# A decoder trunk on one core: forming p's operands in the values' buffers, and multiplying attention's output matrix in two passes

## The chip, the cores and the metric

The kernel runs on one core of one Trainium2 chip. The metric is the device time of one execution in microseconds (us). Three runs of the kernel before took 1282.44, 1286.07 and 1287.14 us; the median is 1286.07 us. The engines are named as the profile names them: PE (TensorE, matmuls) with PEld (its weight loads), DVE (VectorE), ACT (ScalarE), POOL (GpSimd) and SP (SyncE, which here only issues transfers).

## The reference, cut to what matters

Two layers over 512 tokens of width 1024. Layer 0 is a convolution module, layer 1 differential attention; each is followed by a SwiGLU block and by a gated input p of width 256:

```python
for i in range(DEPTH):                                  # 2 layers
    if i % N_MIXERS == 0:
        h = h + conformer_conv(rms_norm(h, conv_norm_g[j]), ...)
    else:
        h = h + diff_attention(rms_norm(h, attn_norm_g[j]), w_qkv, ..., w_o, ...)
    h = h + swiglu(rms_norm(h, ffn_norm_g[i]), w_gate, w_up, w_down)
    gate = sigmoid(rms_norm(h, ple_norm_g[i]) @ ple_w_gate[i])
    h = h + gate * (p[i] @ ple_w_proj[i])
```

The change lies between the two middle lines of layer 1: the end of `diff_attention`, whose last step is `o.reshape(B, S, N_HEADS * V_DIM) @ w_o` over eight heads of 128 values, and the product `p[1] @ ple_w_proj[1]`, which depends on nothing else and is kept until the last line.

## The kernel before, in words

Activations lie transposed: `h[c]` is a tile of 128 features by 512 tokens, c = 0 to 7. Each product of fp32 numbers is made of three matmuls (`mm3`, L161 to L165): both operands are split into a rounded part `hi` and a rest `lo`, and lo*hi, hi*lo and hi*hi are summed in PSUM. A weight tile goes through `weight()` (L144): SP loads 128 x 1024 numbers (512 KB) into one of two raw buffers (`wraw`), ACT rounds them into `whi` (L156), DVE subtracts to get `wlo` (L158); `whi` and `wlo` have four buffers each.

Layer 1's attention is laid out as six slabs of 512 weight columns (`QKV`: q and k of a pair of heads together, or the values of four heads), each multiplied with four blocks of 128 tokens. Between these matmuls stand the pieces of the attention itself. A block (head, qb) has three of them: `stage_s` (scores into `sc`, L944 and L945, then minimum and bias on DVE, L947, and exp on ACT, L951), `stage_t` (transposes, L964, split on ACT and DVE, L966 and L967) and `stage_a` (times the values, L980 and L981). After a head's fourth block its output is normalised in a tile `D`, and `stage_o` transposes it (L1009) and splits it into the tiles `A` (L177, L178) as operand `ot[head]`. After each token block of a q slab, `unit_end` transposes q and k (L899) and splits them (L907 to L917). The values' splits lie in `B0` to `B7`: `B0` to `B3` hold heads 0 to 3, one tile for each token block, `B4` to `B7` heads 4 to 7. q and k of a pair of heads lie in `C0` to `C5`, two buffers each.

33 of the 96 pieces are left when the last slab ends. They are taken one by one by `step()`. First, p is loaded into the two raw buffers and split into `C0` and `C1` (`pfeatures`, L261 and L262; these buffers become free with the scores of heads 4 and 5); two weight tiles and 48 matmuls give the eight products `pp[m]`, evicted by L275 into `D2`, `D3`, `C2`, `C3` and `C4`, with a `step()` at 24 places. Then `linear` multiplies the output matrix: output tiles m = 0 and 1 together, the others one by one, each over all eight heads; `heads_until(k)` first finishes head k, and `add_attn` (L1077) adds to `h[m]` and prepares the next norm. After it comes the SwiGLU of layer 1.

The source sets only what depends on what. The order on each engine is made by a list scheduler with its own estimate of durations (`schedule_with_timeline_sim=True`), and each engine then runs its instructions in that order. DMA issues stand in SP's queue in such an order too, and one that waits for a buffer holds up those behind it.

Of the kernel before, what the change touches and what calls it, by code (L numbers as in the profile page):

```python
# [13 lines left out]
F32R = mybir.dt.float32r  # L14
AF = mybir.ActivationFunctionType
ALU = mybir.AluOpType
# [4 lines left out]
P = 128  # L21
S = 512
D = 1024
NC = D // P
# [67 lines left out]
def trunk(ctx, tc, xT, pT, wts, diag, dww, vec, rel, onehot, lamv, out):  # L92
    nc = tc.nc
    V, A, G, T = nc.vector, nc.scalar, nc.gpsimd, nc.tensor
# [7 lines left out]
    def sb(shape, tag, bufs, dt=F32):  # L102
        uid[0] += 1
        return pool.tile(shape, dt, tag=tag, name=f"{tag}_{uid[0]}", bufs=bufs)

    def ps(tag, bufs, shape=(P, S)):
        uid[0] += 1
        return psum.tile(list(shape), F32, tag=tag, name=f"{tag}_{uid[0]}", bufs=bufs)

    mm = lambda: ps("mm", 4)  # L110
# [4 lines left out]
    f = lambda ap: ap.bitcast(F32)  # L115
# [16 lines left out]
    t = wk()[:, 0:P]  # L132
# [4 lines left out]
    t = tp()  # L137
# [4 lines left out]
    wnext = [0]  # L142
# [18 lines left out]
    def mm3(acc, a, b, first, last):  # L161
        (ah, al), (bh, bl) = a, b
        T.matmul(acc, al, bh, start=first, stop=False)  # L163
        T.matmul(acc, ah, bl, start=False, stop=False)  # L164
        return T.matmul(acc, ah, bh, start=False, stop=last)  # L165

    def wpart(w, k):
        return tuple(t[:, k * P : (k + 1) * P] for t in w)

    def both(t):  # L170
        return t[:, 0], t[:, 1]


    h = [sb([P, S], f"h{c}", 1) for c in range(NC)]
# [82 lines left out]
    def pfeatures(layer, parts):  # L257
        for k, (hi, lo) in enumerate(parts):
            raw = sb([P, 1024], "wraw", 2)[:, :S]
            nc.sync.dma_start(raw, pT[layer, :, k * S : (k + 1) * S])  # L260
            A.copy(hi, raw)  # L261
            (G if layer == 0 else V).tensor_tensor(lo, raw, f(hi), ALU.subtract)  # L262
        return parts

    ph = pfeatures(0, [(sb([P, S], t, 2, F32R), sb([P, S], t, 2, F32R)) for t in ("wth", "wtl")])
# [3 lines left out]
    def project(ph, m, w, o, step=lambda: None):  # L269

        acc = mm()
        for k in range(2):
            last_product[0] = mm3(acc, wpart(w, 2 * (m % 4) + k), ph[k], k == 0, k == 1)
            step()
        A.copy(o, acc)  # L275
        return o
# [4 lines left out]
    accs = {}  # L281
# [206 lines left out]
    pp = []  # L488
# [57 lines left out]
    def linear(n_in, src, consume, group0=1, before=None, after=None, first=(None,) * 3):  # L546


        m = 0
        while m < NC:  # L550
            g = group0 if m == 0 else 1
            ws = [weight(n_in * P, after=first[i] if m == 0 else None) for i in range(g)]
            accs = [mm() for _ in range(g)]
            for k in range(n_in):
                if before:
                    before(k)
                for w_, a_ in zip(ws, accs):
                    mm3(a_, wpart(w_, k), src[k], k == 0, k == n_in - 1)
                    if after:
                        after()  # L560
            for i in range(g):
                consume(m + i, accs[i])
            m += g
# [245 lines left out]
    for k in range(2):  # L809
        t = tp()  # L810
# [193 lines left out]
    ot = {}  # L1004
# [18 lines left out]
    def take(n):  # L1023
        got, stages[:n] = [s for _, s in stages[:n]], []
        return got

    waiting = None
    for what, at, pace in QKV:
        ws = slab(GLO if at > 0 else 0)
        for tb in range(4):  # L1030
            between = take(3 * pace[tb])
            between += [None] * (6 - len(between))
            if waiting:
                between.append(partial(unit_end, *waiting))
                waiting = None
            if what == "v":
                values(at, ws, tb, between)
            else:
                waiting = unit(at, ws, tb, between)
# [5 lines left out]
    def step():  # L1045
        if stages:
            n, s = stages.pop(0)
            s()
        else:
            n = 99  # L1050
        while done[0] < NH and (n - LA - 3) // 4 > done[0]:
            stage_o(done[0])
            done[0] += 1

    ph = pfeatures(1, [both(sb([P, 2, S], t, 2, F32R)) for t in ("C0", "C1")])
    pp = []
    for m in range(NC):
        if m % 4 == 0:
            w = weight()
        step()  # L1060
        if m < 2:
            o = sb([P, S], f"D{m + 2}", 1)
        elif m % 2 == 0:
            o2 = sb([P, 2, S], f"C{m // 2 + 1}", 2)
            o = o2[:, 0]
        else:
            o = o2[:, 1]
        pp.append(project(ph, m, w, o, step))

    def heads_until(k):  # L1070
        while done[0] <= k:
            step()
# [3 lines left out]
    def add_attn(m, acc):  # L1076
        V.tensor_tensor(h[m], acc, h[m], ALU.add)  # L1077
        norm.chunk(m)

    linear(NC, ot, add_attn, 2, heads_until, step)  # L1080
    n2 = Norm("ple_g1")
    ffn(norm, n2, SPACE[1])

# [131 lines left out]
```

## Time and profile before

| | |
|---|---|
| median of three runs | 1286.07 us |
| the profiled execution | 1285.64 us |
| its span, first to last instruction | 1283.8 us |
| PE / DVE / ACT / POOL busy | 98% / 71% / 48% / 21% of the span |
| mean granted PE clock | 0.986 |
| last slab's tokens end, on PE | 790.6 us from the span's start |
| first matmul of the output matrix | 829.99 us |
| first matmul of the SwiGLU behind it | about 884 us |

Times inside the execution are us from the start of the span. A row of a timeline gives start, duration, engine, line, operation and tiles, and at its end in brackets how long the engine sat idle before and what ended that. A matmul's duration covers its way through the array, so matmuls that follow each other start closer together than they last. A row of the table by stretches gives, for each engine, the busy time in that stretch, then the PE clock that was granted (1.00 is full speed), the share of the DMA engines' time and GB/s.

### The profile page before, as it was taken

How to read it: one execution, taken by the hardware profiler on the slowest of the kernel's cores; microseconds unless marked ns; L12 is line 12 of the kernel's file. 1: busy time of each engine (PE TensorE's matmuls, PEld its weight loads, DVE VectorE, ACT ScalarE, POOL GpSimd, SP SyncE). 2: the span in 40 equal slices, each digit the busy share in tenths (PEclk: the TensorE clock that was granted, in tenths of full speed). 3: DMA queues.
4: the chain of work that ended last, by engine and by line, in shares of the span. 5: the costliest groups of instructions: out<-in, count | busy, mean ns of one | idle time of the engine just before them, and what ended most of it. 6: DMA issues, size and time to landing. Idle time of an engine off the chain costs nothing. (4 is left out here: it accounts for less than half of the span.)

```text
span 1283.8 us, 18407 instructions
## 1 busy us (share of the span) xinstructions
PE 1253.2 (98%) x7056; PEld 1089.0 (85%) x7056; DVE 910.9 (71%) x1470; ACT 614.0 (48%) x1019; POOL 273.5 (21%) x239
## 2 busy tenths in 40 slices
PE   8999899999999999999999998999999999999998
PEld 5888678889899989988788886778888899899887
DVE  6888646785578557776678897946974588558665
ACT  5542445443255325454566766834542355235442
POOL 4645323000000000033335544122000001000030
PEclk8999989999999999999999999999999999999999
DMA  6654313275457545233222221313364466444241
GB/s 236 223 163 158 114 48 115 70 209 142 117 143 187 151 119 137 70 121 101 77 92 87 85 76 51 94 49 120 118 169 139 122 176 173 138 110 118 79 140 66
DMA packets 60164, 157.32 MB, mean 123 GB/s; under 512 B 6403, under 2 KB 11011, under 8 KB 60076
## 3 DMA queue, kind: packets, MB, share of 16 engines
q1 hardware_dynamic: 53344, 135.94, 33.2%
q0 software_dynamic: 4608, 16.78, 8.0%
q10 hardware_dynamic: 2124, 3.43, 0.9%
q8 instruction: 55, 0.90, 0.3%
q14 instruction: 33, 0.27, 0.1%
HBM read 151.91 MB, written 4.21 MB: 122 GB/s over the span
## 5 line engine op out<-in xcount | busy, mean ns | idle before, releaser
L164 PE MATMUL mm<-A,whi 128*128 128x512 f32 (+1 forms) x904 | 312.7, 347 | 0.6 <-DVE A L178 0.3
L163 PE MATMUL mm<-A,wlo 128*128 128x512 f32 (+1 forms) x904 | 308.3, 346 | 4.5 <-DVE wlo L158 2.5
L165 PE MATMUL mm<-A,whi 128*128 128x512 f32 (+1 forms) x904 | 310.0, 344 | 0.0
L156 ACT CAST whi<-wraw 128x1024 fp32r<-128x1024 f32 (+2 forms) x150 | 151.2, 1014 | 233.0 <-PE mm L165 93.4
L158 DVE TENSOR_TENSOR wlo<-wraw,whi 128x1024 fp32r<-128x1024 f32 (+2 forms) x146 | 186.6, 1280 | 65.8 <-ACT whi L156 65.0
L163 PEld LDWEIGHTS mm<-A,wlo 128*128 128x128 f32 x904 | 171.8, 190 | 27.5 <-DVE wlo L158 4.2
L164 PEld LDWEIGHTS mm<-A,whi 128*128 128x128 f32 x904 | 172.1, 190 | 24.5 <-DVE A L178 3.8
L165 PEld LDWEIGHTS mm<-A,whi 128*128 128x128 f32 x904 | 172.1, 190 | 20.4 <-issue 1.0
L164 PE MATMUL mm<-B,whi 128*128 128x512 f32 x352 | 137.3, 391 | 0.0
L650 POOL DMA_DIRECT2D C<-in_wts x32 | 28.1, 880 | 511.4 <-DVE h L761 179.4
L165 PE MATMUL mm<-B,whi 128*128 128x512 f32 x352 | 137.1, 390 | 0.0
L163 PE MATMUL mm<-B,wlo 128*128 128x512 f32 x352 | 134.9, 392 | 0.0
L197 POOL TENSOR_TENSOR acc<-acc,wk 128x512 f32<-128x512 f32 x42 | 65.7, 1564 | 229.6 <-ACT wk L196 122.1
L761 DVE TENSOR_TENSOR h<-mm,h 128x512 f32<-128x512 f32 x48 | 33.0, 687 | 64.8 <-PE mm L165 64.8
L165 PEld LDWEIGHTS mm<-B,whi 128*128 128x128 f32 x352 | 66.1, 188 | 14.4
L163 PEld LDWEIGHTS mm<-B,wlo 128*128 128x128 f32 x352 | 66.1, 188 | 14.0
L164 PEld LDWEIGHTS mm<-B,whi 128*128 128x128 f32 x352 | 66.1, 188 | 13.9
L165 PE MATMUL mm<-whi,A 128*128 128x512 f32 x192 | 75.7, 395 | 0.0
L164 PE MATMUL mm<-wlo,A 128*128 128x512 f32 x192 | 74.9, 395 | 0.0
L163 PE MATMUL mm<-whi,A 128*128 128x512 f32 x192 | 74.8, 396 | 0.0
L222 POOL TENSOR_TENSOR r<-v,mhalf 128x8 f32<-128x8 f32 (+1 forms) x31 | 46.2, 1490 | 117.1 <-DVE v L220 94.6
L643 DVE TENSOR_TENSOR wlo<-wraw,whi 128x1024 fp32r<-128x1024 f32 x32 | 39.2, 1225 | 32.8 <-ACT whi L642 32.8
(269 smaller groups left out, 2700.7 us busy)
## 6 DMA issues: line engine op xcount, KB each, us to landing
wraw<-in_wts SPq DMA_DIRECT2D x162, 512.0 KB, 3.7
C<-in_wts SPq DMA_DIRECT2D x32, 512.0 KB, 4.7
C<-in_wts POOLq DMA_DIRECT2D x32, 512.0 KB, 6.2
bias<-in_wts SPq DMA_DIRECT2D x32, 256.0 KB, 3.8
wraw<-in_wts SPq DMA_DIRECT2D x16, 384.0 KB, 3.1
D<-in_diag SPq DMA_DIRECT2D x22, 256.0 KB, 4.2
C<-in_diag SPq DMA_DIRECT2D x16, 256.0 KB, 4.4
h<-in_xT SPq DMA_DIRECT2D x8, 256.0 KB, 5.2
```

The costliest lines, as they stand in the source:

```text
L156: A.copy(hi[:, cut], raw[:, cut])
L158: eng.tensor_tensor(lo[:, cut], raw[:, cut], f(hi[:, cut]), ALU.subtract)
L163: T.matmul(acc, al, bh, start=first, stop=False)
L164: T.matmul(acc, ah, bl, start=False, stop=False)
L165: return T.matmul(acc, ah, bh, start=False, stop=last)
L197: self.last = self.eng.tensor_tensor(self.acc, self.acc, sq, ALU.add)
L222: last_pow[0] = G.tensor_tensor(r[:, :n], v[:, :n], mhalf[:, :n], ALU.pow)
L643: V.tensor_tensor(lo, raw, f(hi), ALU.subtract)
L650: nc.gpsimd.dma_start(q, wts[i + 2].rearrange("p (a s) -> p a s", a=2), accum_op=ALU.add)
L761: V.tensor_tensor(h[m], acc, h[m], ALU.add)
```

## The change

Three things are done.

1. `pfeatures(1, ...)` is called in the last slab, before its third token block, with `B0` and `B1` as the tiles; the values of heads 0 to 3 there are no longer read then.
2. The first four products `pp[0]` to `pp[3]` are evicted into `B2` and `B3`. After attention, DMAs copy them to `D2`, `D3` and `C2`, where the other products of the old kernel lay.
3. The output matrix is multiplied in two passes of half weight tiles (128 x 512 numbers, 256 KB, `half_weight`): first all eight m over heads 0 to 3, with `step()` after each of the 32 products, each m ending in an addition to `h[m]`; then pairs of m over heads 4 to 7, with the old `add_attn`. The numbers of matmuls are the same; weight loads, casts and splits are 16 halves rather than eight whole tiles, and there are eight additions to `h[m]` more.

```diff
@@ -1028,6 +1028,8 @@
     for what, at, pace in QKV:
         ws = slab(GLO if at > 0 else 0)
         for tb in range(4):
+            if (what, at, tb) == ("q", 3, 2):
+                ph = pfeatures(1, [both(sb([P, 2, S], t, 1, F32R)) for t in ("B0", "B1")])
             between = take(3 * pace[tb])
@@ -1052,20 +1054,14 @@
-    ph = pfeatures(1, [both(sb([P, 2, S], t, 2, F32R)) for t in ("C0", "C1")])
     pp = []
     for m in range(NC):
         if m % 4 == 0:
             w = weight()
         step()
-        if m < 2:
-            o = sb([P, S], f"D{m + 2}", 1)
-        elif m % 2 == 0:
-            o2 = sb([P, 2, S], f"C{m // 2 + 1}", 2)
-            o = o2[:, 0]
-        else:
-            o = o2[:, 1]
-        pp.append(project(ph, m, w, o, step))
+        if m % 2 == 0:
+            o2 = sb([P, 2, S], f"B{m // 2 + 2}", 1) if m < 4 else sb([P, 2, S], f"C{m // 2 + 1}", 2)
+        pp.append(project(ph, m, w, o2[:, m % 2], step))
@@ -1077,7 +1073,43 @@
-    linear(NC, ot, add_attn, 2, heads_until, step)
+    base = wnext[0]
+    wnext[0] += NC
+
+    def half_weight(m, first):
+        raw = sb([P, 1024], "wraw", 2)[:, :S]
+        nc.sync.dma_start(raw, wts[base + m, :, first : first + S])
+        hi = sb([P, 1024], "whi", 4, F32R)[:, :S]
+        lo = sb([P, 1024], "wlo", 4, F32R)[:, :S]
+        A.copy(hi, raw)
+        V.tensor_tensor(lo, raw, f(hi), ALU.subtract)
+        return hi, lo
+
+    for m in range(NC):
+        w = half_weight(m, 0)
+        acc = mm()
+        for k in range(4):
+            heads_until(k)
+            mm3(acc, wpart(w, k), ot[k], k == 0, k == 3)
+            step()
+        V.tensor_tensor(h[m], acc, h[m], ALU.add)
+    for m in range(0, NC, 2):
+        ws = [half_weight(m + i, S) for i in range(2)]
+        accs = [mm() for _ in range(2)]
+        for k in range(4):
+            heads_until(4 + k)
+            for w, acc in zip(ws, accs):
+                mm3(acc, wpart(w, k), ot[4 + k], k == 0, k == 3)
+        for i in range(2):
+            add_attn(m + i, accs[i])
+    for m in (0, 1):
+        o = sb([P, S], f"D{m + 2}", 1)
+        nc.sync.dma_start(o, pp[m])
+        pp[m] = o
+    o2 = sb([P, 2, S], "C2", 2)
+    for m in (2, 3):
+        nc.sync.dma_start(o2[:, m % 2], pp[m])
+        pp[m] = o2[:, m % 2]
     n2 = Norm("ple_g1")
     ffn(norm, n2, SPACE[1])
```

What becomes of the order, at three places. The first is PE just behind the last slab's tokens: the scores of head 5's last block (`sc` with 512 columns), and then, before,

```order
L944 MATMUL sc_7575<-C_1193_6468,C_1191_6466 128x512
L945 MATMUL sc_7575<-C_1195_6470,C_1191_6466 128x512
L964 MATMUL tp_7426<-ident_65,big_7250 128x128
L899 MATMUL tp_7444<-ident_65,big_7383 128x128 x4
L944 MATMUL sc_7606<-C_1351_7192,C_1349_7190 128x128
L945 MATMUL sc_7606<-C_1353_7194,C_1349_7190 128x128
```

and with the change

```order
L944 MATMUL sc_7575<-C_1193_6468,C_1191_6466 128x512
L945 MATMUL sc_7575<-C_1195_6470,C_1191_6466 128x512
L163 MATMUL mm_7565<-B_1385_7344,wlo_7500 128x512
L164 MATMUL mm_7565<-B_1385_7344,whi_7499 128x512
L165 MATMUL mm_7565<-B_1385_7344,whi_7499 128x512
L964 MATMUL tp_7436<-ident_65,big_7250 128x128
L899 MATMUL tp_7454<-ident_65,big_7393 128x128 x4
L980 MATMUL mm_7595<-B_1274_6873,wth_7438 128x256
L163 MATMUL mm_7598<-B_1384_7343,wlo_7500 128x512
L164 MATMUL mm_7598<-B_1384_7343,whi_7499 128x512
```

Three of p's matmuls stand ahead of these two pairs of scores and three behind them, twelve more follow the L980 row; before, these 18 stood behind head 0's transposes (L1009), which come after head 6's first scores. The order of the scores and transposes of head 6 between them is nearly kept.

The second place is DVE, from the last step of head 5's fourth block (L956) on. Before:

```order
L956 SCALAR_TENSOR_TENSOR big_7572<-rb_7578,st_7246,big_7572 128x512
L158 TENSOR_TENSOR wlo_7500<-wraw_7498,whi_7499 128x1024
L998 TENSOR_TENSOR v_1415_7516<-v_1415_7516,r_1416_7518 128x4
L954 RECIPROCAL st_7605<-st_7605 128x1
L158 TENSOR_TENSOR wlo_7718<-wraw_7716,whi_7717 128x1024
L947 ISA big_7647,st_7605<-sc_7644,bias_7603 128x256
```

With the change:

```order
L956 SCALAR_TENSOR_TENSOR big_7572<-rb_7578,st_7246,big_7572 128x512
L998 TENSOR_TENSOR v_1415_7516<-v_1415_7516,r_1416_7518 128x4
L947 ISA acc_7613,st_7604<-sc_7605,bias_7602 128x128
L947 ISA st_7604 128x1
L220 TENSOR_SCALAR v_1417_7522<-v_1415_7516 128x4
L954 RECIPROCAL st_7604<-st_7604 128x1
L955 SCALAR_TENSOR_TENSOR st_7604<-st_7604,lam_5566 128x1
L956 SCALAR_TENSOR_TENSOR big_7608<-acc_7613,st_7604,big_7608 128x128
```

The splits of p's two weight tiles have left this place: the first now stands between the two scores with 384 columns of head 5's third block, the second behind the next `unit_end`'s four splits (L915 and L917), with half 0 of the output matrix (L1085) two rows on. The two whole tiles of the output matrix that stood a few rows further down are gone; half 1 stands before the third `unit_end`'s splits, half 2 not before head 6's scores are done.

The third place is SP's queue from p's loads on. Before, p is followed by p's weights and then by the whole tiles. With the change:

```order
L1081 DMA wraw_8079<-in_wts 128x512
L1111 DMA C_1641_8397<-B_1451_7638 128x512
L1107 DMA D_1639_8393<-B_1431_7564 128x512
L1107 DMA D_1640_8395<-B_1431_7564 128x512
L654 DMA bias_8940<-in_wts 128x512
L1111 DMA C_1641_8397<-B_1451_7638 128x512
L1081 DMA wraw_8099<-in_wts 128x512
L1081 DMA wraw_8119<-in_wts 128x512
L654 DMA bias_9069<-in_wts 128x512
L1081 DMA wraw_8139<-in_wts 128x512
```

These are the fourth half, the four copies of the products, a first load for the SwiGLU (L654, into a `bias` buffer that head 6's scores read), the fifth and sixth half, a second such load (into head 7's `bias`) and the seventh half. The copies and the second L654 are new ahead of halves.

## The prediction

> **What bounds the kernel now.** First the page: PE is busy nearly throughout, and its clock is full but for a few slices.
>
> ```profile
> span 1283.8 us, 18407 instructions
> PE 1253.2 (98%) x7056; PEld 1089.0 (85%) x7056; DVE 910.9 (71%) x1470; ACT 614.0 (48%) x1019; POOL 273.5 (21%) x239
> PEclk8999989999999999999999999999999999999999
> ```
>
> So the change can win only where PE waits or runs slowly between the last slab (tokens end at 790.6 us) and the SwiGLU (884). Second, that stretch cut into pieces:
>
> ```profile
> core 0: us, PE busy (x) PEld busy (x) DVE busy (x) ACT busy (x) POOL busy (x), PEclk, DMA share, GB/s
> 792.00:797.00 5.00, 2.21 (x12) 1.30 (x10) 4.89 (x13) 4.60 (x13) 1.09 (x2) 1.00 0.03 12
> 797.00:807.00 10.00, 6.55 (x21) 5.66 (x22) 9.78 (x27) 6.97 (x17) 4.91 (x5) 0.50 0.67 199
> 807.00:818.00 11.00, 9.07 (x51) 6.92 (x50) 10.30 (x28) 8.85 (x20) 1.96 (x1) 0.99 0.40 125
> 818.00:842.00 24.00, 24.00 (x144) 21.09 (x143) 18.62 (x59) 15.68 (x40) 3.62 (x4) 1.00 0.22 67
> 842.00:856.00 14.00, 13.79 (x73) 11.60 (x72) 4.10 (x10) 2.71 (x6) 2.53 (x3) 1.00 0.00 1
> 856.00:862.00 6.00, 3.47 (x17) 2.39 (x15) 3.92 (x6) 3.86 (x6) 0.05 (x1) 1.00 0.00 0
> ```
>
> From 792 to 818 DVE is busy 24.97 of 26 us: there it sets the pace, while PE gets gaps and for ten us half its clock. From 818 to 856 PE is full; at 856 to 862 it waits again. Third, PE's waits of 790 to 862:
>
> ```profile
> PE sc L944 <- DVE st L947: 4.2, 4, 1.7
> PE sc L944 <- DVE st L955: 2.5, 1, 2.5
> PE mm L163 <- DVE wlo L158: 1.8, 1, 1.8
> PE tp L899 <- DVE C L917: 1.0, 1, 1.0
> PE mm L163 <- ACT A L177: 0.8, 1, 0.8
> PE mm L981 <- DVE wtl L967: 0.2, 1, 0.2
> PE sc L944 <- POOL C L912: 0.2, 1, 0.2
> ```
>
> 7.9 us of them (L944, L899) are the front gap; 2.8 us (L163, L981) the tail. Fourth, the chain of waits through the front:
>
> ```profile
> 795.99 0.60 DVE C L262
> 796.62 4.20 DMA wraw<-in_wts
> 800.84 1.06 ACT whi L156
> 801.92 0.43 DVE wlo L158
> ```
>
> p sat in both raw buffers until its split at 796; only then could p's weights load. This work fell due in the middle of the front gap, on an engine already full.
>
> **Front: DVE's relief.** DVE's groups from 790 to 818, and where DVE stands idle earlier:
>
> ```profile
> L158 DVE TENSOR_TENSOR wlo<-wraw,whi 128x1024 fp32r<-128x1024 f32 x4 | 5.2, 1291 | 0.4 <-ACT whi L156 0.4
> L262 DVE TENSOR_TENSOR C<-wraw,C 128x512 fp32r<-128x512 f32 x2 | 1.4, 680 | 0.0
> 771.17 0.69 DVE L947 CUSTOM_DVE_ANT_0 rb<-sc,bias 128x512 f32<-128x512 f32 x1 [1.07 <-PE sc L945]
> 772.56 0.29 DVE L947 CUSTOM_DVE_ANT_0 big<-sc,bias 128x128 f32<-128x128 f32 x1 [0.70 <-PE sc L945]
> 788.72 0.48 DVE L915 SCALAR_TENSOR_TENSOR C<-tp,lam,C 64x256 fp32r<-64x256 f32 x1 [1.41 <-ACT C L908]
> ```
>
> p's two splits move to about 772, where these idle times (1.07 and 0.70) take most of their 1.4 us; PE has the slab's tokens to do there. I cost it at nothing, at 1.4 us if that cover is gone. Of the four whole-tile splits, the first of p's falls into the 1.41 at 788. The second stays (1.3), two whole tiles of the output matrix go (2.6), and two halves come, at 0.68 each by L262, which has their shape (1.4). DVE loses 1.4 + 5.2 - 1.3 - 1.4 = 3.9 us, so what starts at 817.4 starts at 813.5. **-3.9**; at the least 0, if something else turns out to pace the stretch, at the most the 7.9 of waits.
>
> **Front: PE's clock.** The 18 matmuls of p that filled PE at 803 to 810 now stand at 792 to 799. From there to 813 PE has only head 6's scores and four heads' transposes. Thin work already cost it the clock: 2.21 busy us of 5 at 792, then 0.50. Before, the slow matmuls hid behind a DVE that was full (9.78 of 10). Now the clock may still be low when PE has dense work again, where nothing hides it. What that takes:
>
> ```profile
> 803.47 0.78 PE L163 MATMUL mm<-C,wlo 128*128 128x512 f32 x1
> 807.37 0.40 PE L165 MATMUL mm<-C,whi 128*128 128x512 f32 x1
> 817.38 0.39 PE L163 MATMUL mm<-C,wlo 128*128 128x512 f32 x1
> 819.90 0.39 PE L165 MATMUL mm<-C,whi 128*128 128x512 f32 x1
> 156.00:172.00 16.00, 15.99 (x50) 12.48 (x50) 4.65 (x11) 4.97 (x11) 1.96 (x2) 0.50 0.12 33
> ```
>
> Twelve products at full clock start 2.52 us apart from first to last, 0.229 each. From 803.47 to 807.37 PE did eight such and two small ones: 3.9 us for about 2.0. I take **+1.9**, since the low spell that began the same way ended so; at the least 0 (no drop), at the most 8, half of the 16 us for which the other spell held on, dense work or not.
> [...]
>
> **Tail.** Head 7's normalisation ends in L1009, L177 and L178, and PE waited 0.8 us for L177, 0.2 for L967. That chain is this long:
>
> ```profile
> 849.05 0.37 ACT L987 COPY D<-mm 128x256 f32<-128x256 f32 x1 [4.28 <-PE mm L981]
> 853.38 1.04 POOL L1002 TENSOR_TENSOR D<-D,r 128x512 f32<-128x512 f32 x1 [0.36 <-DVE r L1000]
> ```
>
> 5.4 us from head 7's last value matmuls to its transposes. With the change the rest of pass one, which needs heads 0 to 3 only, and the first pair's heads 4 to 6 stand between: 50 matmuls, 11 us by 0.229, and another 17 before the first use of the operand; both waits go. The 1.8 us for L158 had this cause: four tiles wait for head 7, so all four `whi` buffers are held, and the next weight is split only when one is done.
>
> ```profile
> 858.83 0.94 DVE h L1077 x2
> 860.63 1.23 DVE wlo L158
> L1077 DVE TENSOR_TENSOR h<-mm,h 128x512 f32<-128x512 f32 x4 | 2.6, 684 | 1.0 <-PE mm L165 1.0
> ```
>
> That remains: pass two again holds four halves until head 7 is there. But ahead of the split now stand two additions rather than three (0.6 less), and the split is a half (1.23 - 0.68 = 0.55 less): 1.1 of 1.8 goes. **-2.1** (0.2 + 0.8 + 1.1); bounds 0 and -2.8.
>
> **Added work.** Eight more additions (8 x 0.684 = 5.5 us) and 16 halves for eight tiles (16 x 0.68 - 8 x 1.23 = 1.0 us) on DVE lie in the first pass, where DVE was busy 4.10 of 14 us: nothing; 6.5 if all of it were exposed. The additions wait for PE's m, and behind them in DVE's queue stand splits for three m's later and head 7's L994 to L1000; these have the 11 us above. On SP the copies wait for products 2 and 3 and for the transposes of heads 2 and 3, all of which stand ahead of head 7's first scores on PE; the second L654 waits for head 7's last scores, which stand inside the first m. Behind them wait halves five and seven, due four and six m's (11 and 16 us by 0.229) after pass one's start. Nothing, or one landing:
>
> ```profile
> wraw<-in_wts SPq DMA_DIRECT2D x162, 512.0 KB, 3.7
> bias<-in_wts SPq DMA_DIRECT2D x32, 256.0 KB, 3.8
> h<-in_xT SPq DMA_DIRECT2D x8, 256.0 KB, 5.2
> L261 ACT CAST C<-wraw x2: 637/638/638, 792.7 to 793.2; 128x512 fp32r<-128x512 f32 x2
> ```
>
> A half lands no sooner than a whole tile (3.8 against 3.7). A raw buffer is held 3.8 + 0.64 + 0.68 = 5.1 us, two give a half every 2.6 us, and PE uses one in 12 x 0.229 = 2.75: just enough.
>
> **Sum**: -3.9 + 1.9 - 2.1 = -4.1, against the profiled execution's 1285.64 (its span and 1.8 around it; 0.4 below the median of the runs, 1286.07): **1281.5 us**, 0.3% faster. Less than 0.5% (6.4 us) can't be told from no change here, so this forecast counts as the same.
>
> **Rivals.** (a) The gap closes: p's matmuls and the lighter DVE take PE's whole front wait and the clock holds. For it: the 18 matmuls are as long (4.1 us) as half the wait. Against: DVE stays full by the sum above. At its limit 1285.64 - 7.9 - 2.1 = 1275.6.
> (b) The low clock lasts, as at 156 to 172: 1285.64 - 3.9 + 8 - 2.1 = 1287.6, slower than before. Place: the first dense matmuls behind 813; each us there loses half; from 12 us of it on the 6.0 gained are spent. For it that spell; against it 807, where four us of work sufficed.
> (c) Halves come too slowly: at a landing of 5.2, a raw buffer is held 6.5, a half comes every 3.3 us, 0.5 late. Over the twelve behind the first four that is 6 us, if the four split ahead give no lead: 1287.5. It decides from a landing of 4.2 (2 x 2.75 - 1.32). For it: eight more transfers on one queue. Against: 818 to 862 moves little (67 GB/s and less).
> (d) The change doesn't do at the front what it says: the chain PE, DVE, ACT of head 6's scores paces it, not DVE's load. Only the tail is won: 1285.64 - 2.1 = 1283.5. For it: L944 waits for one score after another; against: DVE's 96%.
> (e) DVE's relief comes as summed, and the clock stays full: 1285.64 - 3.9 - 2.1 = 1279.6. For it: from 807 to 818 PE was 82% busy (9.07 of 11), waits between, at clock 0.99. Against: the five us at 792, which are nearer to the thin work that is left. [...]
>
> **Chances.** Forecast 0.40 (its own range 1279 to 1284), (a) 0.14, (b) 0.12, (c) 0.09, (d) 0.11, (e) 0.14. The range 1275.5 to 1288.5 reaches from (a)'s limit past (b) and (c); outside lie the clock's and DVE's far bounds together. Faster by over 0.5% needs 1279.6: (a), half of (e) and the forecast's near edge, 0.26. Slower by over 0.5% needs 1292.5: (b) or (c) with the front's gain missing too, 0.08. Same 0.66.
>
> **What would show it.** Right: p's first matmul near 792 and dense PE work from about 813.5; DVE still over 90% busy in the stretch; a slow spell reaching into the dense work by about four us; no PE wait for L177 or L967 at head 7 and under one us for L1085. Wrong: PE waiting for `wlo` in pass one or two (c), full clock throughout (a, e), dense work from 817 again (d).

## The result, and the profile after

The changed kernel took 1287.86 us (median of 22 runs, 1284.39 to 1293.72) beside 1284.78 us of the kernel before (22 runs). The ratio is 1.0023, with a 95% interval of 1.0013 to 1.0033: 3 us slower, where 0.3% faster was forecast. The time lies inside the forecast's range, but the change went the other way, clear of the noise. The profiled execution took 1288.40 us. In the ratios further down, one execution each of e3_tail and e8_p_early_nostep, far above the others (2678 and 1373 us), is left out. From the profile's page:

```profile
span 1286.6 us, 18474 instructions
PEclk8999989999999999999999999799999999999999
```

The 26th digit of the clock's row, the slice from 804 us on, has gone from 9 to 7. Where the 3 us lie is told by two rows that both kernels have: the first score on DVE, and the last addition behind layer 1's first half of the SwiGLU. Before,

```profile
650.95 0.29 DVE L947 CUSTOM_DVE_ANT_0 big<-sc,bias 128x128 f32<-128x128 f32 x1
1015.34 0.69 DVE L761 TENSOR_TENSOR h<-mm,h 128x512 f32<-128x512 f32 x1 [2.18 <-PE mm L165]
```

and with the change

```profile
650.71 0.29 DVE L947 CUSTOM_DVE_ANT_0 big<-sc,bias 128x128 f32<-128x128 f32 x1
1018.04 0.69 DVE L761 TENSOR_TENSOR h<-mm,h 128x512 f32<-128x512 f32 x1 [2.18 <-PE mm L165]
```

That is 364.39 us before and 367.33 after: +2.94, as much as the two spans differ by (2.8). Below this stretch is called the segment. The table by stretches, with the cuts of the prediction's:

```profile
792.00:797.00 5.00, 3.33 (x18) 2.58 (x17) 4.91 (x12) 4.07 (x11) 0.55 (x2) 1.00 0.34 105
797.00:807.00 10.00, 6.29 (x31) 5.15 (x29) 8.28 (x32) 7.42 (x21) 6.63 (x8) 0.84 0.25 79
807.00:818.00 11.00, 9.05 (x36) 6.73 (x35) 8.97 (x25) 6.56 (x16) 0.00 (x0) 0.53 0.13 49
...
856.00:862.00 6.00, 6.00 (x28) 4.95 (x27) 3.33 (x9) 1.25 (x2) 2.05 (x2) 1.00 0.26 87
862.00:876.00 14.00, 13.38 (x61) 10.76 (x60) 7.10 (x9) 7.00 (x13) 2.73 (x2) 1.00 0.19 56
876.00:884.00 8.00, 4.98 (x22) 3.80 (x21) 7.18 (x8) 1.72 (x4) 3.95 (x4) 1.00 0.27 75
```

DVE (third busy time) is no longer full from 797 to 818, the low clock has moved from 797 to 807 into 807 to 818 (0.53), and PE, full at 856 to 862 where it had waited, now waits at 876 to 884. PE's waits from 785 to 890 by what they waited for:

```profile
PE mm L163 <- DVE wlo L1085: 3.6, 2, 3.0
PE sc L944 <- DVE st L947: 2.7, 2, 2.1
PE tp L899 <- DVE C L917: 1.7, 1, 1.7
PE tp L1009 <- DVE C L917: 1.0, 1, 1.0
PE sc L944 <- DVE v L220: 1.0, 1, 1.0
PE mm L980 <- ACT wth L966: 0.8, 2, 0.5
PE tp L964 <- DVE A L178: 0.4, 1, 0.4
PE mm L163 <- DVE wlo L158: 0.2, 1, 0.2
```

The sum of the loss, by idle time of PE in the stretches and by busy time times the missing part of the clock (in windows of 0.5 us):

| | before | after | difference |
|---|---|---|---|
| PE idle, 790.6 to 818 | 8.17 | 7.33 | -0.8 |
| PE idle, 818 to 900 | 2.74 | 4.23 | +1.5 |
| PE busy at the low clock, lost part | 3.4 | 5.5 | +2.1 |
| sum | | | +2.8 of 2.94 |

The low clock of this execution lasts from 803.5 to 817.5, and it ends where the dense work begins (products that follow each other without waits, the first at 817.7):

```profile
803.50:817.50 14.00, 11.44 (x45) 8.64 (x44) 10.82 (x33) 8.58 (x22) 2.49 (x4) 0.51 0.10 39
817.50:821.00 3.50, 3.50 (x21) 2.99 (x20) 2.99 (x9) 3.13 (x9) 0.00 (x0) 1.00 0.23 77
```

The new wait of the tail is this one. The last pair of half tiles is multiplied 3.02 us late; first PE's row, then DVE's and POOL's:

```profile
880.34 0.50 PE L163 MATMUL mm<-A,wlo 128*128 128x512 f32 x1 [3.02 <-DVE wlo L1085]
```

```profile
873.25 3.49 DVE L178 SCALAR_TENSOR_TENSOR A<-h,vec,A 128x512 fp32r<-128x512 f32 x2
...
874.96 3.46 DVE L178 SCALAR_TENSOR_TENSOR A<-h,vec,A 128x512 fp32r<-128x512 f32 x2
878.35 0.68 DVE L1073 TENSOR_TENSOR h<-mm,h 128x512 f32<-128x512 f32 x1
878.95 0.73 DVE L178 SCALAR_TENSOR_TENSOR A<-h,vec,A 128x512 fp32r<-128x512 f32 x1
879.61 2.37 DVE L1085 TENSOR_TENSOR wlo<-wraw,whi 128x512 fp32r<-128x512 f32 x2
873.19 4.68 POOL L197 TENSOR_TENSOR acc<-acc,wk 128x512 f32<-128x512 f32 x3 [13.60 <-ACT wk L196]
879.83 1.60 POOL L197 TENSOR_TENSOR acc<-acc,wk 128x512 f32<-128x512 f32 x1 [1.96 <-ACT wk L196]
```

(The first two rows overlap in one instruction: three of L178 run from 873.25 to 878.4.) Each takes 1.7 us while POOL adds the squares (L197), and 0.73 alone at 878.95. The last pair's weight splits (L1085) stand behind them.

### The profile page after: what moved, and what is told of

Its sections match the earlier page's. It is cut to its first block, busy times and chain, and to the rows that moved or that the text cites. A ratio compares the mean times of both kernels' runs of the same rounds, so it can differ in the third digit from the quotient of the medians.

```text
span 1286.6 us, 18474 instructions
## 1 busy us (share of the span) xinstructions
PE 1254.7 (98%) x7056; PEld 1089.7 (85%) x7056; DVE 915.5 (71%) x1486; ACT 615.5 (48%) x1027; POOL 273.2 (21%) x239
## 4 chain that ended last, share of the span: by engine, by line
PE 80%; DVE 8%; DMA 3%; ACT 3%; issue 3%; POOL 2%; SPq 1%; ACTq 0%; DVEq 0%; POOLq 0%
PE mm L163 22%; PE mm L164 21%; PE mm L165 21%; PE tp L165 2%; PE tp L164 2%; PE tp L163 2%; DVE wlo L158 1%; DVE sc L401 1%; PE sc L164 1%; PE sc L163 1%; PE sc L165 1%; POOL wk L389 1%; DMA wraw<-in_wts 1%; DMA po<-big 1%; PE mm L980 1%
## 5 line engine op out<-in xcount | busy, mean ns | idle before, releaser
L156 ACT CAST whi<-wraw 128x1024 fp32r<-128x1024 f32 (+2 forms) x142 | 142.7, 1012 | 218.3 <-DMA wraw<-in_wts 88.6
L158 DVE TENSOR_TENSOR wlo<-wraw,whi 128x1024 fp32r<-128x1024 f32 (+2 forms) x138 | 175.9, 1277 | 59.7 <-ACT whi L156 59.3
L164 PE MATMUL mm<-B,whi 128*128 128x512 f32 x368 | 143.6, 391 | 0.0
L165 PE MATMUL mm<-B,whi 128*128 128x512 f32 x368 | 143.4, 391 | 0.0
L163 PE MATMUL mm<-B,wlo 128*128 128x512 f32 x368 | 141.2, 392 | 0.0
L197 POOL TENSOR_TENSOR acc<-acc,wk 128x512 f32<-128x512 f32 x42 | 66.3, 1578 | 227.8 <-ACT wk L196 119.8
L165 PEld LDWEIGHTS mm<-B,whi 128*128 128x128 f32 x368 | 69.1, 188 | 15.1
L163 PEld LDWEIGHTS mm<-B,wlo 128*128 128x128 f32 x368 | 69.2, 188 | 14.5
L164 PEld LDWEIGHTS mm<-B,whi 128*128 128x128 f32 x368 | 69.1, 188 | 14.4
```

The lines of the kernel that those rows point to most:

```text
L156: A.copy(hi[:, cut], raw[:, cut])
L158: eng.tensor_tensor(lo[:, cut], raw[:, cut], f(hi[:, cut]), ALU.subtract)
L197: self.last = self.eng.tensor_tensor(self.acc, self.acc, sq, ALU.add)
```

## The experiments

All ratios are against the kernel before, run on the same chip in turn. "Low spell" is the time at a clock below 0.97, read in windows of 0.5 us; the segment is the one above.

### One part at a time

The first kernel (e1_p_early) has the change's hunks on `pfeatures` and on the products, with the copies, but the old output matrix; the second (e2_two_pass) has the two passes alone.

The first, against the changed kernel:

```diff
-    for m in range(NC):
-        w = half_weight(m, 0)
...
+    linear(NC, ot, add_attn, 2, heads_until, step)
```

and the second:

```diff
-            if (what, at, tb) == ("q", 3, 2):
-                ph = pfeatures(1, [both(sb([P, 2, S], t, 1, F32R)) for t in ("B0", "B1")])
...
+    ph = pfeatures(1, [both(sb([P, 2, S], t, 2, F32R)) for t in ("C0", "C1")])
```

> Only p is moved (formed in the last slab into B0 and B1, first four products in B2 and B3, copies at the end); the output matrix is multiplied in one pass of whole tiles as before. Theory A (from the two traces: the front gap changes by -0.8 us of waits and +2.1 us of slow clock, and p's move does both; the tail's +1.5 us belongs to the two passes): 1.3 us slower than before, about 1.0010 of it, a low clock between 803 and 818 and the old tail waits on L158 and L177 (2.6 us). Theory B (the two passes cause the whole loss, p's move frees DVE as predicted): 2 to 4 us faster than before, 0.997 to 0.9985. Theory C (the copies on SP's queue hold up weights): slower by more than 2 us, with PE waits on weights behind the copies.

> Only the two passes of half tiles; p is formed behind the last slab in C0 and C1 as before. Theory A (two passes take away the waits for L177 and L967 and bring a longer one for the last pairs' splits, p's move has the rest): 1.5 us slower than before, 1.0012, with a PE wait of about 3 us for the last pair's split and the low clock at 797 to 807 as before. Theory B (two passes gain in the tail as predicted when p is not in the way): 2.1 us faster, 0.9984. Theory D (front and tail are coupled, halves instead of whole tiles relieve DVE in the front gap): front waits fall by over 2 us, 0.998 or less.

Measured: p's move alone 0.9989 (0.9974 to 1.0003), 1282.85 us; the two passes alone 1.0005 (0.9991 to 1.0019), 1284.86 us. Neither is told from no change by itself. Their sum, 0.9994, lies below the 1.0023 of both, but each has an interval of some 0.0014 either way, and p's move once more gave 1.0004 (at the end of the experiments): that the parts cost more together than apart isn't shown. Nor do the times decide between theories A and B for p's move, since the first run leaves out A's 1.0010 and the second one B's 0.9985. PE's waits of p's move:

```profile
PE sc L944 <- DVE st L947: 4.0, 2, 3.4
PE mm L163 <- DVE wlo L158: 1.8, 1, 1.8
PE tp L1009 <- DVE C L917: 1.4, 1, 1.4
PE tp L899 <- DVE C L917: 1.3, 1, 1.3
PE mm L163 <- ACT A L177: 0.8, 1, 0.8
...
```

Its front waits hardly change (`sc`, `tp` and three smaller rows left out here make 8.1 us, against 7.9 before), and the tail's two rows (L158, L177) are the old ones. So the waits that B would take away are still there, and theory C falls: the copies hold up nothing. Of the two passes:

```profile
PE mm L163 <- DVE wlo L1089: 3.6, 2, 3.0
```

(L1089 is L1085 there.) The 3.0 us wait comes with the two passes, p's place apart, as theory A has it; and where the prediction had taken 2.1 us off the tail (theory B), it is longer. In the profiled execution that wait was followed by a low spell of 7 us (877.5 to 884.5), which cost 3.0 us more.

### The tail's order on DVE

In this kernel (e3_tail) `last_half[0]` is the last pair's split, and `tc.issue_after` holds an instruction behind another in the scheduler's order:

```diff
-    def split_scaled(src, scale, hi, lo):
+    def split_scaled(src, scale, hi, lo, behind=None):
         A.activation(hi, src, AF.Copy, scale=scale)
-        V.scalar_tensor_tensor(lo, src, scale, f(hi), ALU.mult, ALU.subtract)
+        with tc.issue_after(behind.ins) if behind else nullcontext():
+            V.scalar_tensor_tensor(lo, src, scale, f(hi), ALU.mult, ALU.subtract)
...
     def add_attn(m, acc):
         V.tensor_tensor(h[m], acc, h[m], ALU.add)
-        norm.chunk(m)
+        if m >= 4:
+            norm.chunk(m)
...
+    nxt = [half_weight(i, S) for i in range(2)]
     for m in range(0, NC, 2):
-        ws = [half_weight(m + i, S) for i in range(2)]
+        ws = nxt
...
+        if m + 2 < NC:
+            nxt = [half_weight(m + 2 + i, S) for i in range(2)]
+        if m == NC - 4:
+            for c in range(4):
+                norm.chunk(c, last_half[0])
         for i in range(2):
             add_attn(m + i, accs[i])
```

> The changed kernel, but DVE may form the next norm's operand for the first four chunks of h only behind the split of the last pair of half tiles, whose load is issued one pair ahead. Theory A (the 3.0 us wait of the last pair is made by DVE's order: three of the norm's splits, slowed to 1.7 us each beside POOL's additions, ahead of the weight's split): the wait falls below 0.6 us and the time by 2.5 to 3 us against the changed kernel, to 0.9997 to 1.0005 of the kernel before. Theory E (the half tiles land too late in any order, a raw buffer being free only at 871.5): the wait stays over 1.5 us, the gain is below 1.5 us. Theory F (the norm's splits then hold up the first SwiGLU matmuls instead): the wait moves behind 886 and the time stays at 1.0023.

Measured: 1.0000 (0.9987 to 1.0013), 1285.56 us. The front's order is unchanged, and so are its low spell (14 us) and its lost clock (5.54 us); the segment falls from 367.33 to 365.15, -2.2. PE's rows (L1087 is L1085 there):

```profile
868.72 0.50 PE L163 MATMUL mm<-A,wlo 128*128 128x512 f32 x1 [0.62 <-DVE wlo L1087]
881.30 0.50 PE L163 MATMUL mm<-A,wlo 128*128 128x512 f32 x1 [1.40 <-DVE wlo L158]
```

The 3.02 us are gone; 1.40 of them come back at the first weight of the SwiGLU (theory F, for a part), since the norm's splits must be done before it too. The edit also asks for each pair of half tiles one pair earlier (`nxt`), so the gain alone doesn't tell the order on DVE (A) from the landing (E). The changed kernel's own trace does. There ACT had rounded both halves of the last pair by 876.4, before PE ran out of work at 877.3, and DVE began their splits only at 879.61:

```profile
875.29 1.12 ACT L1084 CAST whi<-wraw 128x512 fp32r<-128x512 f32 x2
```

So the order of DVE's queue made the wait (A), not the landing (E).

### p's products close together

The kernel e4_nostep:

```diff
         if m % 4 == 0:
             w = weight()
-        step()
...
-        pp.append(project(ph, m, w, o2[:, m % 2], step))
+        pp.append(project(ph, m, w, o2[:, m % 2]))
```

> The changed kernel, but p's eight products are not interleaved with pieces of the attention (no step among them); the pieces go between the products of pass one. The 48 matmuls of p then stand close together from 791 on, and pass one starts earlier among head 6's blocks. Theory A (the front gap is thin work on PE waiting for head 6's chain, and the low clock follows from it): with denser work the clock stays full or the low spell shrinks below 3 us of busy time, front waits fall from 7.3 us to below 4; 4 to 6 us faster than the changed kernel, 0.998 of the kernel before. Theory G (the chain of head 6's and head 7's pieces sets the end of attention, whatever PE does meanwhile): the pieces are only later, waits move to 830 to 860, and the time is that of the changed kernel or above, 1.002 to 1.006.

Measured: 0.9963 (0.9948 to 0.9978), 1280.67 us, over 7 us below the changed kernel. The stretch from 790.6 to 818 of the changed kernel, and then of this one:

```profile
790.60:818.00 27.40, 20.07 (x91) 15.71 (x90) 23.53 (x67) 19.39 (x48) 7.49 (x10) 0.75 0.20 68
```

```profile
790.60:818.00 27.40, 25.01 (x123) 20.03 (x122) 21.82 (x58) 19.18 (x47) 7.22 (x10) 0.94 0.30 96
```

PE is busy 25.0 of 27.4 us instead of 20.1, at 0.94 of the clock instead of 0.75: one low piece of 3.5 us is left. What PE lacked was work that does not hang on the chain, and it was in the program all along: in the changed kernel 30 of p's 48 matmuls stood behind pieces of heads 6 and 7. Theory A holds, with a gain above its 4 to 6 us and a spell a little over its 3 us, and G falls.

The same with e3_tail's edit as well (e5_nostep_tail):

> p's products without pieces among them (as e4_nostep) and the next norm's first four splits behind the last pair's weight split (as e3_tail), both in the changed kernel. Theory A (the two losses are separate: front thin work, tail order on DVE): e4's wait of 2.1 us for the last pair's split goes, at most a wait of 1.4 us for the first SwiGLU weight comes instead as in e3_tail; 0.7 to 2.1 us faster than e4_nostep, 0.9947 to 0.9957 of the kernel before. Theory F (the tail's wait only moves to the next weight): equal to e4_nostep, 0.9963.

Measured: 0.9944 (0.9928 to 0.9959), 1278.24 us: 7 us faster than the kernel before, and the fastest seen. The front has no low spell at all (its tail has one of 4 us, from 875 to 879):

```profile
790.60:818.00 27.40, 24.72 (x127) 19.89 (x127) 22.22 (x62) 19.11 (x47) 6.37 (x8) 1.00 0.26 85
```

The wait for the last pair is gone; 2.4 us at the first SwiGLU weight stand in its place, more than the 1.4 expected. Its segment (360.21) differs from e4_nostep's (360.49) by only 0.3, so the 2.4 us between the medians is mostly not the tail's; whether the mend adds to the dense order stays open.

And dense products without the two passes (e8_p_early_nostep, e1_p_early with the edit of e4_nostep):

> p formed early in B0 and B1, its products without pieces among them, and the output matrix in one pass of whole tiles as before (e1_p_early plus the edit of e4_nostep). Theory A (dense products in the front gap bring the gain and the two passes none): front waits below 4 us and at most one low piece as in e4_nostep, tail waits as in the kernel before; 0.9945 to 0.9965 of it. Theory I (with one pass the pieces of heads 6 and 7 find no cover behind p, because the output matrix needs all eight heads by its first two tiles: two passes are what makes the dense order possible): waits of 5 us or more between 815 and 850, 0.998 to 1.003.

Measured: 1.0003 (0.9991 to 1.0014), 1285.68 us. That is theory I by the time: the front is filled (23.84 of 27.4 us), but the thin work only comes later. From 815 to 850 PE is idle for 4.0 us rather than the 5 expected, and a low spell from 835.5 to 843 costs 3.1 us more:

```profile
824.00:836.00 12.00, 8.61 (x54) 6.79 (x52) 11.28 (x41) 7.53 (x23) 2.28 (x2) 1.00 0.07 24
836.00:850.00 14.00, 13.39 (x63) 11.31 (x63) 4.80 (x12) 3.75 (x9) 2.05 (x2) 0.76 0.00 0
```

A pass over eight heads has nothing to cover heads 6 and 7 with, as its first two output tiles need them. So, with p formed early, the two passes and the dense products give the gain together, and neither does alone (1.0023 and 1.0003). No run has both with p formed late, so what p's early place adds to the gain stays open.

### DVE's load by itself

Three kernels measure the prediction's first term. In the first POOL takes over 3.9 us of DVE's splits in the kernel before; in the second they are left out; in the third 2.7 us of splits are left out of the changed kernel. The first (e6_before_pool), with `eng0=G` for the output matrix alone:

```diff
-            (G if layer == 0 else V).tensor_tensor(lo, raw, f(hi), ALU.subtract)
+            G.tensor_tensor(lo, raw, f(hi), ALU.subtract)
...
-            ws = [weight(n_in * P, after=first[i] if m == 0 else None) for i in range(g)]
+            ws = [weight(n_in * P, eng=(eng0 or V) if m == 0 else V, after=first[i] if m == 0 else None) for i in range(g)]
```

> The kernel before, with 3.9 us of DVE's work in the front gap given to POOL and nothing else moved by hand: p's two splits (0.68 us each on DVE) and the splits of the output matrix's first two tiles (1.23 each). It measures the prediction's first term by itself. Prediction's term (DVE's load paces 792 to 818): the front waits fall from 8.2 us to about 4.3, the dense work starts at 813.5, 3 to 4 us faster, 0.997. Rival (the chain of head 6's scores and the transposes of its q and k paces it, each step waiting for one small result, and DVE's load only sits beside it): front waits stay between 7 and 9 us, 0.9992 to 1.0010. A POOL split lasts 1.3 to 1.7 us for 512 columns and 2.4 for 1024, so slower than that would mean p's weight waits for POOL.

Measured: 1.0017 (1.0002 to 1.0031), slower. It tells little of DVE, since POOL's own pieces come late behind its splits; POOL, and then PE:

```profile
804.96 4.71 POOL L158 TENSOR_TENSOR wlo<-wraw,whi 128x1024 fp32r<-128x1024 f32 x2 [1.89 <-ACT whi L156]
809.74 0.85 POOL L912 CAST C<-C 64x256 fp32r<-64x256 f32 x2
809.99 0.63 PE L1009 MATMUL tp<-ident,D 128*128 128x128 f32 x4 [2.51 <-DVE C L917]
```

So the work was left out instead (e9_before_nolo), and then in the changed kernel (e9b_after_nolo). The edit is shown for the latter's `half_weight`, where it holds for the first four half tiles; in the kernel before it is the like in `pfeatures` and `weight`:

```diff
         A.copy(hi, raw)
+        if nolo:
+            return hi, hi
         V.tensor_tensor(lo, raw, f(hi), ALU.subtract)
         return hi, lo
...
-        w = half_weight(m, 0)
+        w = half_weight(m, 0, m < 4)
```

> The kernel before, with the same 3.9 us of DVE's work left out of the front gap: the rests of p's two tiles and of the output matrix's first two weight tiles are not computed (the rounded part stands in for the rest, so that PE does the same matmuls on other numbers). In e6_before_pool, POOL's own pieces were late behind the splits; here nothing takes their place. Prediction's term (DVE's load paces the gap): 3 to 4 us faster, front waits near 4.3 us, 0.997. Rival (chain of small results): waits stay at 7 us or more and the time within 1.5 us, 0.9988 to 1.0012, at most the 0.7 to 1.2 us by which p's operand and weight are ready sooner.

Measured: 0.9986 (0.9974 to 0.9998), 1282.56 us; front waits of 5.4 us against 7.9:

```profile
PE sc L947 <- DVE st L950: 3.6, 3, 1.9
PE tp L902 <- DVE C L920: 1.0, 1, 1.0
PE tp L1012 <- DVE A L180: 0.8, 1, 0.8
```

(All lines are 3 higher there.) Between the two theories: 3.9 us of DVE are worth 1.8 us, 0.3 to 3.3 by the interval, the sooner operand of p included. (Its segment in the one trace, 361.85, is 2.5 us below the first trace of the kernel before and 5.3 below the second, which comes last below; so the size rests on the runs.)

> The changed kernel, with the rests of the first four half tiles of the output matrix left out (four DVE splits of 0.68 us, 2.7 us, of which two stand between 792 and 799); the rounded part stands in. If DVE's load sets the front of the changed kernel: 1.4 to 2.7 us faster than it, 1.0002 to 1.0012 of the kernel before. If the chain does: within 1 us of the changed kernel, 1.0015 to 1.0031.

Measured: 1.0015 (1.0002 to 1.0028), 1286.12 us; the segment is 365.41, 1.9 below the changed kernel's, and the low spell 7.5 us instead of 14. The ratio stands at the edge of what was expected if the chain sets the front, the segment inside what was expected of DVE's load, so this run decides neither. Two of those four splits stand at 792 and 797 on DVE. The next kernel (e12_hold) keeps them, but puts all four behind head 6's last score, and e13_hold_tail has this and e3_tail's edit:

```diff
-        V.tensor_tensor(lo, raw, f(hi), ALU.subtract)
+        with tc.issue_after(behind.ins) if behind else nullcontext():
+            V.tensor_tensor(lo, raw, f(hi), ALU.subtract)
...
-        w = half_weight(m, 0)
+        w = half_weight(m, 0, scored[6, 3] if m < 4 else None)
```

> The changed kernel, but DVE may split the first four half tiles of the output matrix only behind head 6's last score (about 817 us); in the changed kernel two of these splits stand at 792 and 797, though PE first uses them at about 829. Nothing is left out. Theory J (these early splits delay head 6's chain and so lengthen the low spell; leaving them out gave 2 us): the low spell falls from 14 us to 7 to 10.5 and the time by 1.5 to 2.5 us against the changed kernel, 1.0005 to 1.0013 of the kernel before. Theory K (the gain came from the work that was left out, wherever it stands): within 0.8 us of the changed kernel, 1.002 or more.

Measured: 1.0011 (1.0002 to 1.0021), 1286.37 us; the low spell is 7.5 us, and the segment 366.47, 0.9 below the changed kernel's. By the ratios the time is 1.5 us below the changed kernel's, at the near edge of theory J (1.5 to 2.5); the intervals overlap, so it is likely rather than shown that the place of these splits counts and not their work.

> Both mends of DVE's order in the changed kernel: the early splits behind head 6's last score, and the next norm's splits behind the last pair's weight splits. If the two are separate and are all that turned the change's gain into a loss: 3 us (as from e3_tail) and 1.5 to 2.5 us (theory J) below the changed kernel, 1282.5 to 1284, 0.998 to 0.9993 of the kernel before, about what moving p alone gave. If something else in the two passes costs time: 1.0000 or more.

Measured: 1.0005 (0.9993 to 1.0018), 1285.44 us. Both mends of order bring the change back to the kernel before; the 0.998 to 0.9993 that separate gains would make isn't reached. Next to e3_tail (1.0000) the runs show nothing more won, though the segment in the one trace is 1.1 us shorter (364.09). With intervals of 0.0013 either way, whether the early splits' 1.5 us add to the tail's stays open.

### The low clock

The kernel e7_twice, with `TWICE = (6,)`; the transposes of `stage_o` for heads 0 to 3 are repeated in the same way:

```diff
+            for _ in range(1 if hd in TWICE else 0):
+                T.matmul(acc[:, :n], qs[c][:, i, cut], ks[c][:, i, 0:n], start=True, stop=False)
+                T.matmul(acc[:, :n], qs[c][:, i, cut], kl[c][:, i, 0:n], start=False, stop=True)
             T.matmul(acc[:, :n], qs[c][:, i, cut], ks[c][:, i, 0:n], start=True, stop=False)
...
-            T.transpose(t[:, k * P : (k + 1) * P], w_[:, k * P : (k + 1) * P], ident)
+            for _ in range(2 if hd in TWICE else 1):
+                T.transpose(t[:, k * P : (k + 1) * P], w_[:, k * P : (k + 1) * P], ident)
```

> The changed kernel, with PE's thin work between 799 and 818 done twice: head 6's scores, head 6's transposes and the transposes of heads 0 to 3 are each issued a second time into the same place (some 7 us more of PE's time in all, most of it where PE would wait). Theory A (the low clock of 803 to 817 comes from the share of time in which PE works): the low spell shrinks from 14 us to one 3.5 us piece or none, the lost clock from 5.5 us to below 2; added work that is not hidden costs 1 to 4 us, so the time lies between 2 us faster and 1 us slower than the changed kernel (1.0008 to 1.0031 of the kernel before). Theory H (the low clock comes from waits between matmuls, however much stands between them, or from anything else): a spell of 10 us or more stays, and the doubled work runs at half clock: 3 us or more slower than the changed kernel, 1.0047 or more.

Measured: 1.0043 (1.0027 to 1.0059), 1290.98 us. The clock does what theory A says: the low spell of the front falls from 14 us to 4 and the lost clock from 5.5 to 1.7. From 807 to 818, where the changed kernel had 0.53:

```profile
807.00:813.00 6.00, 4.53 (x32) 4.00 (x32) 5.22 (x14) 3.22 (x7) 0.00 (x0) 1.00 0.11 43
813.00:818.00 5.00, 4.40 (x26) 3.52 (x25) 4.43 (x14) 3.79 (x10) 0.00 (x0) 1.00 0.14 53
```

But the second issue of each piece stands in the chain itself and costs more than the clock gives back: 2.6 us slower than the changed kernel, by the medians' ratios, outside A's -2 to +1. (A second spell of 4 us, in the tail from 881.5 on, cost this execution 1.7 us too.) Where PE has more to do in the front the spell is shorter, here and in e4_nostep and e5_nostep_tail; but each of these is one execution, and the next runs show how far executions of one kernel can differ, so it is likely rather than shown that the clock follows PE's work. Buying it with work inside the chain didn't pay.

Last, the changed kernel, the kernel before and e1_p_early once more, without an edit, for other profiled executions:

> The changed kernel once more, for a second profiled execution on the chip of these runs. If the changed order itself makes the low clock longer: again three or four pieces of 3.5 us between 800 and 818, and 1286.5 to 1289 us. If the number of pieces is drawn by chance in each execution: another number than four, with the same waits, and a span that differs by about 1.7 us for each piece.

> The kernel before once more, for a second profiled execution of it. Same order: the front waits are again about 8 us and the tail's 2.8 us. If its low spell belongs to the order: three pieces of 3.5 us from about 797; if by chance: two or four.

> Only p moved, once more (as e1_p_early), for a second profiled execution beside e12 and e13 on the same chip. If p's move alone keeps the low spell short because of its order: two pieces of 3.5 us again between 798 and 818, and 1282 to 1284 us. If that was chance: three or four pieces, and a time nearer to the kernel before.

Measured: the changed kernel 1.0027 (1.0011 to 1.0044), p's move alone 1.0004 (0.9991 to 1.0018), the kernel before 1.0004 against itself. The changed kernel's segment repeats to the hundredth: it is 367.33 again, with the same waits, and the low spell again about 14 us, though the whole stretch lies 3.3 us earlier:

```profile
800.00:814.50 14.50, 11.94 (x47) 9.08 (x47) 11.15 (x35) 9.09 (x24) 2.64 (x4) 0.53 0.10 37
```

The kernel before doesn't repeat: segment 367.14 against 364.39, with a low spell of 7 us, a pause, and another of 7.5 (4.8 us lost, against 3.4), and 9.5 us of front waits, against 7.9:

```profile
PE sc L944 <- DVE st L947: 5.8, 4, 2.5
PE sc L944 <- DVE st L955: 2.5, 1, 2.5
```

p's move alone had 3.5 + 4 us in one execution and 17.5 us in the other (segments 363.22 and 365.10). So the two pairs of traces give +2.9 and +0.2 us for the change, and the runs +3.0 (first result) and +3.5: the sign and the size stand on the runs, and a single pair of traces tells which terms there are, not what the clock costs on the mean of the runs.

Outside the segment the clock varies as well. The spell at 156 to 172 that the prediction shows lasts 17.5 us in the first traces of both kernels, with PE busy 15.99 and 16.00 of the 16 us, and 7 us in e10_after_again and e11_before_again. So PE's share of work can't be all that decides; what else does, no run here tells.

## Why the prediction was wrong

**What bounds the stretch** was read half right. DVE was 96% busy from 792 to 818, and taking work off it does help, but at less than its price: 3.9 us left out are worth 1.8, at most 3.3 (e9_before_nolo). A busy engine in a chain of small steps (score, minimum, exp, transpose) is not the pace by itself; when DVE has air, PE still waits for `st` and `C`, one after another.

**DVE's relief, -3.9**: this step failed. The changed kernel has air on DVE (8.28 of 10 us and 8.97 of 11, against 9.78 and 10.30), though from 792 to 818 it is 2.8 us, not 3.9. But PE's idle time in the front only fell from 8.17 to 7.33, -0.8, and dense work started at 817.7, not at 813.5. Rival (d) named this: the chain of head 6's scores sets the pace.

**PE's clock, +1.9**: the size was right by luck (+2.1 in this pair of traces, +0.8 in the other), the place wrong. No dense work ran slowly: the low spell ended at 817.5 with the first dense matmuls. It lay in the thin stretch before, where for 14 us PE's steps of the chain ran at 0.51 of the clock. So the two front terms may not be two: the thin work that was to be the price of the earlier p may also be what kept DVE's relief from reaching the dense work. That fits these rows and e4_nostep, but no run shows it by itself. Rival (b), 1287.6, came nearest to 1287.86, but by its name only, since its half-speed dense work isn't there; that the time lies inside the range is luck for the same reason. Rival (e) fails: the clock didn't stay full, but fell to 0.51 at 803.5, with no wait above 2.1 us ahead of it.

**Tail, -2.1**: this step failed too, by sign: +1.5. What was named went: no wait for L177 or for `wtl` at head 7, and none for a half tile in pass one or in the first two pairs of pass two. But the sum stopped at head 7. Behind it the scheduler put the next norm's splits ahead of the last pair's weight splits on DVE, and POOL's additions of the squares, which run at the same time, stretched them from 0.73 to 1.7 us. In the kernel before, all splits of the output matrix's weights stood ahead of the norm's first splits, which come at 880.87:

```profile
879.72 1.23 DVE L158 TENSOR_TENSOR wlo<-wraw,whi 128x1024 fp32r<-128x1024 f32 x1 [0.44 <-ACT whi L156]
880.87 2.46 DVE L178 SCALAR_TENSOR_TENSOR A<-h,vec,A 128x512 fp32r<-128x512 f32 x2
```

e3_tail, with ACT's row beside it, shows it: another order takes the 3.0 us wait away and 2.2 us off the segment. The list of what would show the forecast had "under one us for L1085"; it was 3.6.

**Added work, 0**, was right: no PE wait for a half tile in pass one, none for a copy, none for one of the eight additions. The 16 halves landed in 2.4 to 3.8 us, half of them within 2.6, where the prediction took 3.8 from `bias`; so rival (c) was priced too high. The split that came late, the last pair's, did so for a cause that (c) did not have.

**The sum** was -4.1 and is +2.8 in the first pair of traces. The miss of 6.9 us is made of 3.1 from DVE's relief, 3.6 from the tail and 0.2 from the clock.

What stays open: why the front's low spell is 14 us in all three executions that have the changed kernel's front order (the two above and e3_tail), and between 7 and 17.5 us with p's move alone; and how much of the 3 us is this spell on the mean of the runs.

## What to carry to other kernels

An engine at 96% in a stretch of small dependent steps is no proof that its load sets the pace; leave the same work out, as an experiment, before its microseconds go into a sum. Independent matmuls are worth most where PE has thin work, and the source order that interleaves them with the chain can lock them out: here 48 matmuls taken out of the interleaving, with two passes that give the rest of the chain a cover, turned +0.23% into -0.37%, and the same with the tail's order mended ran at -0.56%. When a loop is cut into two, look at what the scheduler puts between the last loads' splits and their use, as it is the end of the loop that has nothing to hide behind.

## What the runs showed of the hardware

In these executions PE's low clock came in pieces of about 3.5 us. Read in windows of 0.5 us, the low spells, from 140 to 185 us and from 785 to 900, last 3.5, 7, 10.5, 14 or 17.5 us (within 0.5): in the front 10.5 (before), 14 (changed), 7.5 (e12_hold), 3.5 (e4_nostep). How many pieces a thin stretch gets varied from one execution of the same kernel to another: with p's move alone 3.5 + 4 us in one and 17.5 in the other. In the changed kernel PE was busy 6.29 of the 10 us from 797 to 807, in which the clock fell.

In the changed kernel's tail DVE's splits took longer while POOL added. The three of L178 that began during additions of L197 took 5.17 us together, 1.7 each, and the one at 878.95, beside none, 0.73 (rows above). Of the two weight splits of L1085 the first, begun at 879.61, took 0.68, and the second, begun at 880.21 within POOL's addition of 879.83 to 881.43, took 1.77. All of these read two tiles of SBUF; an addition of L1073, which reads one of its operands from PSUM, kept its 0.68 beside POOL's addition of 886.29:

```profile
886.85 0.68 DVE L1073 TENSOR_TENSOR h<-mm,h 128x512 f32<-128x512 f32 x1
886.29 1.80 POOL L197 TENSOR_TENSOR acc<-acc,wk 128x512 f32<-128x512 f32 x1 [1.55 <-ACT wk L196]
```

So a sum of mean durations leaves out a cost that these rows show.
